# Rotary products of branch B on VectorE, inside the wide gate groups

## The chip, the cores and the metric

The kernel runs on one core of one Trainium2 chip. Its time is the device time of one execution in microseconds; beside it stands the span, from the first to the last instruction of the profiled execution.

## The reference

One layer of a hybrid encoder block on a sequence of 512 rows of width 2048. What matters here is the input projection (10,752 columns) and what branch B does with its eight query heads and two key heads of 128 columns: a norm per head, then a rotary embedding along two axes.

```python
h = rmsnorm(x, norm_g[l])
proj = jnp.einsum('bsd,dc->bsc', h, w_in[l])
qa, ka, va, za, qb, kb, vb, zb, ga, gb = jnp.split(proj, SPLIT_POINTS, axis=-1)
...
qb = axial_rope(rmsnorm(qb.reshape(B, S, N_HEADS_B, DH_B), q_norm_g[l]))
kb = axial_rope(rmsnorm(kb.reshape(B, S, N_KV_B, DH_B), k_norm_g[l]))
ob = gqa_attention(qb, kb, vb)
yb = jnp.einsum('bsc,cd->bsd', ob * jax.nn.silu(zb), w_out_b[l])
merged = jax.nn.sigmoid(ga) * ya + jax.nn.sigmoid(gb) * yb
x = x + jnp.einsum('bsd,de->bse', merged, w_o[l])
```

Branch A (differential attention with its own rotary embedding), the output projections and a final norm complete it; all is float32.

## The kernel before

Every float32 product is made from three matmuls on rounded halves: ScalarE casts a piece of weights to `w_hi` (L115), VectorE computes the residual `w_lo` (L116), and TensorE adds hi x hi, lo x hi and hi x lo. Three buffers of each half (`wp`) let the casts run ahead of TensorE. Large products go by a Strassen scheme of seven products on quarters; the sums of weight quarters are VectorE's (`sub`, L220 and L317), the sums of results too (`plus`, L254 and L337).

The stages in order of time: the input is normed, turned and split; a first part of the projection (L248); then, from about 112 to 570 us, six wide groups of 1024 columns (`strassen_wide`, L329): two keep columns in `pv`, a scratch in HBM, four compute the sigmoid gates (L568) and store them in `gg`. From 570.70 to 764.40 us come the SiLU gates: four groups of 512 columns (`strassen`, L248, L657, L658). Then 16 heads with their attention (from about 764 to 1120 us), between whose steps TensorE takes steps of the rest of the projection and of branch B's output projection, as the list `FILLS` says; then the last projections.

`rope_b(n)` treats one head of branch B (n below 8 a query, 8 and 9 the keys): it loads the head's 512x128 columns from `pv`, ScalarE squares and sums them (L616), GpSimd makes the inverse root with two small operations (`rsqrt_pool`, L111 and L112), then multiplies by the tables and adds (L627 to L629), ScalarE scales the key heads by row (L632), and the columns go back to `pv`. `b_table` multiplies the cosines and signed sines with the norm's gains on GpSimd, once for queries and once for keys (L599, L602). Both tables are made at the start of the SiLU gates, and `to_rope` puts the ten ropes behind the four groups: 4, 3, 3 and 0. The order of instructions on an engine's queue is made by a planner that works from modelled durations; each queue then runs in that order. An instruction under `tc.keep_in_program_order` is put behind the one written before it on its engine; what is written later may still pass it. On TensorE the heads' order is written out by hand. All loads and stores are issued by SyncE's queue.

Of the kernel before, what the change touches and what calls it, by code (L numbers as in the profile page):

```python
# [11 lines left out]
F32 = mybir.dt.float32  # L12
F32R = mybir.dt.float32r
AF = mybir.ActivationFunctionType
ALU = mybir.AluOpType
AX = mybir.AxisListType

P = 128
D = 2048
S = 512  # L20
NT = S // P
NK = D // P
BW = 1024
EPS = 1e-6
# [20 lines left out]
WIDE = "0125"  # L45

FILL_FIRST = 6
FILLS = "130 120 130 120 120 130 130 130 130 130 120 231 231 231 231 231".split()


@with_exitstack
def hybrid_block_kernel(
# [8 lines left out]
    nc = tc.nc  # L61
# [16 lines left out]
    def share_banks(**kw):  # L78
        banks.update(kw)
# [29 lines left out]
    def rsqrt_pool(dst, ss, mul, add, n):  # L109

        nc.gpsimd.tensor_scalar(out=dst, in0=ss, scalar1=mul, scalar2=add, op0=ALU.mult, op1=ALU.add)  # L111
        nc.gpsimd.tensor_tensor(out=dst, in0=dst, in1=neg_half[:, :n], op=ALU.pow)  # L112
# [177 lines left out]
        o = [slots[2 * i:2 * i + 2] for i in range(4)]  # L290
        slots[:] = o[1] + o[0] + o[3] + o[2]

    def strassen_wide(w, left, right, act, wide, done, late=False):

        H = NK // 2

        def load(q, half, pieces):  # L300
            tiles = []
            for p in range(4):
                if q < 2:
                    r = raw_tile(q * 4 + p, (2, S))
                else:
                    r = wide.tile([P, 2, S], F32, name="w_raw", tag=f"w_wide{p}")
                row, at = (half * H + p * 2) * P, 0
                for c0, n in pieces:
                    nc.sync.dma_start(out=r[:, :, at:at + n],
                                      in_=w[row:row + 2 * P, c0:c0 + n].rearrange("(k p) n -> p k n", p=P))  # L310
                    at += n
                tiles.append(r)
            return tiles

        def sub(dst, x0, x1):
            for d, u, v in zip(dst, x0, x1):
                nc.vector.tensor_tensor(out=d, in0=u, in1=v, op=ALU.subtract)  # L317

        def product(name, b):
            ps = acc_tile(2, S)  # L320
            ah, al = act[name]
            for p in range(4):
                hi, lo = split_w(b[p])
                for u in range(2):
                    sl = slice(u * P, (u + 1) * P)
                    for k in range(2):
                        kk = p * 2 + k
                        for i, (l, r) in enumerate(((ah, hi), (al, hi), (ah, lo))):
                            nc.tensor.matmul(out=ps[:, u, :], lhsT=l[:, kk, sl], rhs=r[:, k, :],  # L329
                                             start=kk == 0 and i == 0, stop=kk == H - 1 and i == 2)  # L330
            return ps

        def tmp(tag):
            return wide.tile([P, 2, S], F32, name="wide_" + tag, tag="wide_" + tag)

        def plus(dst, ps, sb):
            nc.vector.tensor_tensor(out=dst, in0=ps, in1=sb, op=ALU.add)  # L337
            return dst

        b11, b12 = load(0, 0, left), None  # L340
        if late:
            b12 = load(1, 0, right)
        b21 = load(2, 1, left)
        b12 = b12 or load(1, 0, right)

        p1 = product("a11", b11)
        u = tmp("u")
        nc.scalar.copy(out=u, in_=p1)
        if not late:
            p2 = product("a12", b21)  # L350
            b22 = load(2, 1, right)
        sub(b11, b12, b11)
        p5 = product("s1", b11)
        if late:
            p2 = product("a12", b21)
            b22 = load(2, 1, right)
        done(0, 0, plus(tmp("c"), p2, u))
        sub(b11, b22, b11)
        p6 = product("s2", b11)
        plus(u, p6, u)  # L360
        t = plus(tmp("t"), p5, u)
        sub(b12, b22, b12)
        p3 = product("s3", b12)
        b21 = load(1, 1, left)
        plus(u, p3, u)
        done(1, 1, plus(tmp("c"), p5, u))
        if late:

            ring = banks["acc"]
            ring[0], ring[1] = ring[1], ring[0]  # L370
        done(0, 1, plus(t, product("s4", b22), t))
        sub(b21, b21, b11)
        done(1, 0, plus(u, product("a22", b21), u))
# [21 lines left out]
    written = {}  # L395
# [42 lines left out]
    with tc.tile_pool(name="xs", bufs=1) as xs:  # L438
# [116 lines left out]
        slots[:] = slots[2:4] + slots[0:2] + slots[4:]  # L555
        new_banks("pair")
        share_banks(acc=[2, 3, 0, 1])
        with tc.tile_pool(name="wide", bufs=1) as wide:
            for n, blocks in enumerate(WIDE_BLOCKS):
                def kept(th, ch, v, blocks=blocks):  # L560
                    keep_cols(blocks[ch * 4:ch * 4 + 4], th * 2, 2, v)

                strassen_wide(w_in, column_pieces(blocks[:4]), column_pieces(blocks[4:]), xq, wide, kept, late=n == 0)


            for g in range(0, 2 * D, 2 * S):
                def merge_gate(th, ch, v, g=g):
                    nc.scalar.activation(out=v, in_=v, func=AF.Sigmoid)  # L568
                    c = g + ch * S
                    nc.sync.dma_start(  # L570
                        out=gg[th * 256:th * 256 + 256, c:c + S].rearrange("(u p) n -> p u n", p=P), in_=v)

                strassen_wide(w_in, [(O_GA + g, S)], [(O_GA + g + S, S)], xq, wide, merge_gate)
        slots[:] = slots[0:2] + slots[4:6] + slots[2:4] + slots[6:8]

        with tc.tile_pool(name="sp", bufs=6) as sp:
# [7 lines left out]
            for blocks in STRASSEN_BLOCKS[1:]:  # L584
                project(blocks, tmp, lambda ps: tmp())

            tabs = {}

            def b_table(nm, src):

                g = sp.tile([P, P], F32, name="g_" + nm, tag="g_" + nm, bufs=1)
                nc.sync.dma_start(out=g, in_=src.broadcast_to([P, P]))
                tcb = sp.tile([P, NT, P], F32, name=f"tc_{nm}", tag=f"tc_{nm}", bufs=1)
                tsb = sp.tile([P, NT, P], F32, name=f"ts_{nm}", tag=f"ts_{nm}", bufs=1)
                nc.sync.dma_start(out=tcb, in_=cos_b.rearrange("(t p) c -> p t c", p=P))
                nc.sync.dma_start(out=tsb, in_=sin_b.rearrange("(t p) c -> p t c", p=P))
                gv = g.rearrange("p (h r j) -> p h r j", h=2, r=2)
                for t in range(NT):
                    nc.gpsimd.tensor_tensor(out=tcb[:, t, :], in0=tcb[:, t, :], in1=g, op=ALU.mult)  # L599
                    ov = tsb[:, t, :].rearrange("p (h r j) -> p h r j", h=2, r=2)  # L600
                    for r in range(2):
                        nc.gpsimd.tensor_tensor(out=ov[:, :, r, :], in0=ov[:, :, r, :],  # L602
                                                in1=gv[:, :, 1 - r, :], op=ALU.mult)
                tabs[nm] = tcb, tsb

            def rope_b(n):


                b = B_QB + n if n < 8 else B_KB + n - 8
                assert written[b] == NT  # L610
                v = sp.tile([P, NT, P], F32, name="cols", tag="cols", bufs=4)
                nc.sync.dma_start(out=v, in_=pv[b])
                sq = sp.tile([P, P], F32, name="bsq", tag="bsq", bufs=1)
                ss = rb[:, n, :]
                for t in range(NT):
                    nc.scalar.activation(out=sq, in_=v[:, t, :], func=AF.Square, accum_out=ss[:, t:t + 1])  # L616
                if n < 8:

                    rsqrt_pool(ss, ss, 1.0, P * EPS, NT)
                else:  # L620
                    rsqrt_pool(ss, ss, 1.0 / P, EPS, NT)
                t2 = sp.tile([P, NT, P], F32, name="rope2", tag="rope2", bufs=1)
                tcb, tsb = tabs["q" if n < 8 else "k"]
                for r in range(2):
                    d, s, m = (x.rearrange("p t (a r j) -> p t a r j", r=2, j=32)[:, :, :, q, :]
                               for x, q in ((t2, r), (v, 1 - r), (tsb, r)))
                    nc.gpsimd.tensor_tensor(out=d, in0=s, in1=m, op=ALU.mult)  # L627
                nc.gpsimd.tensor_tensor(out=v, in0=v, in1=tcb, op=ALU.mult)  # L628
                nc.gpsimd.tensor_tensor(out=v, in0=v, in1=t2, op=ALU.add)  # L629
                if n >= 8:  # L630
                    for t in range(NT):
                        nc.scalar.mul(out=v[:, t, :], in_=v[:, t, :], mul=ss[:, t:t + 1])  # L632
                nc.sync.dma_start(out=pv[b], in_=v)

            b_table("q", q_norm_g)
            b_table("k", k_norm_g)
            to_rope = [(0, 8, 1, 2), (3, 4, 5), (9, 6, 7), ()]


            nc.sync.dma_start(out=sub_g, in_=subln_g.rearrange("o p -> p o"))  # L640
# [12 lines left out]
            for c0, dst in ((O_ZA, zg[0:BW]), (O_ZB, zg[BW:])):  # L653
                for g in range(0, BW, S):
# [8 lines left out]

                    strassen(w_in, c0 + g, c0 + g + 256, xq, False, tmp, gate)
                    for n in to_rope.pop(0):
                        rope_b(n)

    rest = [i for i in range(8) if i not in banks["acc"]]
    share_banks(acc=rest[:2], aux=rest[2:] + banks["acc"])
# [591 lines left out]
```

## Time and profile before

| what | before |
|---|---|
| median of 3 runs | 1397.26 us (1396.12 to 1399.37) |
| the profiled execution's own time | 1396.01 us |
| its span | 1394.2 us |
| mean granted clock of TensorE | 0.988 |
| TensorE busy | 1344.5 us (96%) |
| VectorE busy | 1069.6 us (77%) |
| ScalarE busy | 711.1 us (51%) |
| GpSimd busy | 218.0 us (16%) |

Busy times are of the profiled execution, on the one core. A stage is read from windows of the span: busy time of each engine, and the clock that TensorE was granted in it (1.00 is 2.4 GHz). A wait is put down to what ended it last.

### The profile page before, as it was taken

The numbers are of one execution on the slowest core, as the hardware profiler recorded it, in microseconds if no ns is written. First come the engines' busy times: TensorE is split into PE (matmuls) and PEld (weight loads), VectorE is DVE, ScalarE is ACT, GpSimd is POOL, SyncE is SP. The second block draws the span as 40 slices with busy tenths as digits, with TensorE's granted clock in tenths as the row PEclk, the third lists the DMA queues.
The fourth block names the chain that finished last, engine by engine and source line by source line (L and its number), as shares of the span: only waits on it lengthen the run. The fifth ranks groups of instructions, "written<-read, shape, count | busy, mean of one in ns | idle before, by whom it ended". The sixth has DMA issues, their size and how long they took to land.

```text
span 1394.2 us, 20919 instructions
## 1 busy us (share of the span) xinstructions
PE 1344.5 (96%) x8009; PEld 1200.2 (86%) x8009; DVE 1069.6 (77%) x1271; ACT 711.1 (51%) x1104; POOL 218.0 (16%) x194
## 2 busy tenths in 40 slices
PE   6999999999999999967999999999999999999997
PEld 5998888888888888867999888888889988899997
DVE  5976978778788787736876477978878856799986
ACT  7643343444444444445444476656767733344444
POOL 1000000000000000399100411432220000004322
PEclk9999999999999999987999999999999999999999
DMA  8254653636272734542446684454754455463333
GB/s 287 76 149 134 195 187 116 216 93 240 86 262 91 249 113 146 164 152 98 159 152 173 199 247 129 138 165 144 220 167 153 131 169 187 140 221 112 96 103 121
DMA packets 182756, 222.38 MB, mean 159 GB/s; under 512 B 12016, under 2 KB 126976, under 8 KB 182016
## 3 DMA queue, kind: packets, MB, share of 16 engines
q1 hardware_dynamic: 182656, 221.04, 50.1%
q8 instruction: 63, 1.03, 0.3%
q14 instruction: 37, 0.30, 0.1%
HBM read 181.15 MB, written 35.65 MB: 155 GB/s over the span
## 4 chain that ended last, share of the span: by engine, by line
PE 80%; DVE 6%; POOL 5%; DMA 3%; ACT 3%; issue 3%; SPq 0%; POOLq 0%; DVEq 0%; ACTq 0%
PE acc L329 32%; PE acc L186 21%; PE acc L248 19%; PE aux L762 2%; DVE w_lo L116 2%; PE aux L749 1%; PE aux L875 1%; DMA cols<-pv 1%; POOL rope L627 1%; POOL cols L628 1%; PE aux L805 1%; PE aux L806 1%; POOL cols L629 1%; DMA w_raw<-in_w_in_dram 1%; DMA xt<-in_x_dram 1%
## 5 line engine op out<-in xcount | busy, mean ns | idle before, releaser
L115 ACT CAST w_hi<-w_raw 128x1024 fp32r<-128x1024 f32 x357 | 375.2, 1052 | 479.1 <-PE acc L329 235.5
L116 DVE TENSOR_TENSOR w_lo<-w_raw,w_hi 128x1024 fp32r<-128x1024 f32 x357 | 453.7, 1275 | 189.3 <-ACT w_hi L115 188.9
L317 DVE TENSOR_TENSOR w_raw<-w_raw 128x1024 f32<-128x1024 f32 x96 | 116.8, 1222 | 23.3 <-DMA w_raw<-in_w_in_dram 22.1
L220 DVE TENSOR_TENSOR w_raw<-w_raw 128x1024 f32<-128x1024 f32 x72 | 94.7, 1315 | 3.4 <-DMA w_raw<-in_w_in_dram 2.5
L599 POOL TENSOR_TENSOR tc_q<-tc_q,g_q 128x128 f32<-128x128 f32 x4 | 4.7, 1201 | 556.8 <-DMA g_k<-in_k_norm_g_dram 556.8
L186 PE MATMUL acc<-w_hi,og1h 128*128 128x256 f32 x256 | 73.5, 287 | 2.0 <-DVE rows L939 2.0
L329 PE MATMUL acc<-w_hi,a2h 128*128 128x512 f32 x192 | 74.7, 389 | 0.0
L329 PE MATMUL acc<-w_hi,a2l 128*128 128x512 f32 x192 | 74.7, 389 | 0.0
L329 PE MATMUL acc<-w_lo,a2h 128*128 128x512 f32 x192 | 74.7, 389 | 0.0
L186 PE MATMUL acc<-w_hi,og1l 128*128 128x256 f32 x256 | 73.2, 286 | 0.0
L186 PE MATMUL acc<-w_lo,og1h 128*128 128x256 f32 x256 | 73.1, 286 | 0.0
L716 DVE TENSOR_REDUCE nmax<-aux 128x1 f32<-128x512 f32 x96 | 61.4, 680 | 5.1 <-PE aux L806 5.1
L704 POOL TENSOR_TENSOR cols<-cols,ca 128x512 f32<-128x512 f32 x16 | 23.0, 1435 | 245.2 <-DMA other<-pv 111.4
L186 PE MATMUL acc<-a1h,w_hi 128*128 128x512 f32 (+1 forms) x160 | 56.9, 361 | 0.4 <-ACT a1h L492 0.2
L186 PE MATMUL acc<-a1l,w_hi 128*128 128x512 f32 (+1 forms) x160 | 56.3, 357 | 0.1
L186 PE MATMUL acc<-a1h,w_lo 128*128 128x512 f32 (+1 forms) x160 | 56.3, 356 | 0.0
L186 PE MATMUL acc<-a2h,w_hi 128*128 128x512 f32 (+1 forms) x160 | 55.6, 350 | 0.0
L186 PE MATMUL acc<-a2l,w_hi 128*128 128x512 f32 (+1 forms) x160 | 55.5, 348 | 0.0
L186 PE MATMUL acc<-a2h,w_lo 128*128 128x512 f32 (+1 forms) x160 | 55.4, 347 | 0.0
L186 PEld LDWEIGHTS acc<-w_hi,og1h 128*128 128x128 f32 x256 | 49.7, 194 | 2.8 <-DVE rows L939 2.2
L186 PEld LDWEIGHTS acc<-w_lo,og1h 128*128 128x128 f32 x256 | 49.7, 194 | 0.6
L186 PE MATMUL acc<-w_hi,og0h 128*128 128x512 f32 x128 | 50.0, 392 | 0.0
(360 smaller groups left out, 4102.2 us busy)
## 6 DMA issues: line engine op xcount, KB each, us to landing
w_raw<-in_w_in_dram SPq DMA_DIRECT2D x160, 512.0 KB, 4.5
w_raw<-in_w_in_dram SPq DMA_DIRECT2D x64, 256.0 KB, 4.3
w_raw<-in_w_o_dram SPq DMA_DIRECT2D x32, 512.0 KB, 3.5
cols<-pv SPq DMA_DIRECT2D x36, 256.0 KB, 4.0
w_raw<-in_w_out_b_dram SPq DMA_DIRECT2D x16, 512.0 KB, 3.8
w_raw<-in_w_out_a_dram SPq DMA_DIRECT2D x32, 256.0 KB, 3.2
xt<-in_x_dram SPq DMA_DIRECT2D x8, 512.0 KB, 7.9
gg<-wide_c SPq DMA_DIRECT2D x8, 512.0 KB, 3.6
```

Source lines behind the costliest of these rows:

```text
L115: nc.scalar.copy(out=hi, in_=src)
L116: nc.vector.tensor_tensor(out=lo, in0=src, in1=hi.bitcast(F32), op=ALU.subtract)
L186: nc.tensor.matmul(out=acc[b][:, place], lhsT=l, rhs=r, start=first and kc == order[0] and k == 0 and i == 0, stop=last and kc == order[-1 ...
L220: nc.vector.tensor_tensor(out=d, in0=u, in1=v, op=ALU.subtract)
L248: nc.tensor.matmul(out=ps[u] if by_row else ps[:, u, :], lhsT=l, rhs=r, start=n % (2 if by_row else 4) == 0 and k == 0 and i == 0, stop=n ...
L317: nc.vector.tensor_tensor(out=d, in0=u, in1=v, op=ALU.subtract)
L329: nc.tensor.matmul(out=ps[:, u, :], lhsT=l[:, kk, sl], rhs=r[:, k, :], start=kk == 0 and i == 0, stop=kk == H - 1 and i == 2)
L627: nc.gpsimd.tensor_tensor(out=d, in0=s, in1=m, op=ALU.mult)
L628: nc.gpsimd.tensor_tensor(out=v, in0=v, in1=tcb, op=ALU.mult)
L704: nc.gpsimd.tensor_tensor(out=v, in0=v, in1=ca, op=ALU.mult)
L716: nc.vector.tensor_reduce(out=nmax, in_=sps, axis=AX.X, op=ALU.max, negate=True)
L762: nc.tensor.matmul(out=o, lhsT=l, rhs=r, start=j == 0 and i == 0, stop=j == NT - 1 and i == 2)
```

## The change

The table for queries and the eight query ropes are moved into the four wide gate groups: in each group one rope stands in the middle (`amid`, after the sum `t` is formed and before the weights of `p3` are summed) and one behind it. Only the table and the two ropes for keys stay in the SiLU gates, one behind each of the first two groups. In all ropes the products and the sum run on VectorE instead of GpSimd. The first of them write the two halves of a tile `rope2` that also takes the squares; the squares and the two first products are kept behind what is written before them on their engine. The columns have one buffer instead of four. The list of fill steps for TensorE between the heads is another, with the same total.

```diff
-FILLS = "130 120 130 120 120 130 130 130 130 130 120 231 231 231 231 231".split()
+FILLS = "120 120 130 120 120 130 130 120 120 131 131 231 231 231 231 231".split()
...
     def strassen_wide(w, left, right, act, wide, done, late=False, amid=None):
...
         t = plus(tmp("t"), p5, u)
+        if amid:
+            amid()
         sub(b12, b22, b12)
         p3 = product("s3", b12)
...
+        def rope_b(sp, n):
+            b = B_QB + n if n < 8 else B_KB + n - 8
+            assert written[b] == NT
+            v = sp.tile([P, NT, P], F32, name="cols", tag="cols", bufs=1)
+            nc.sync.dma_start(out=v, in_=pv[b])
+            t2 = sp.tile([P, NT, P], F32, name="rope2", tag="rope2", bufs=1)
+            ss = rb[:, n, :]
+            for t in range(NT):
+                tc.keep_in_program_order(
+                    nc.scalar.activation(out=t2[:, t, :], in_=v[:, t, :], func=AF.Square, accum_out=ss[:, t:t + 1]))
+            if n < 8:
+                rsqrt_pool(ss, ss, 1.0, P * EPS, NT)
+            else:
+                rsqrt_pool(ss, ss, 1.0 / P, EPS, NT)
+            tcb, tsb = tabs["q" if n < 8 else "k"]
+            for r in range(2):
+                d, s, m = (x.rearrange("p t (a r j) -> p t a r j", r=2, j=32)[:, :, :, q, :]
+                           for x, q in ((t2, r), (v, 1 - r), (tsb, r)))
+                tc.keep_in_program_order(nc.vector.tensor_tensor(out=d, in0=s, in1=m, op=ALU.mult))
+            nc.vector.tensor_tensor(out=v, in0=v, in1=tcb, op=ALU.mult)
+            nc.vector.tensor_tensor(out=v, in0=v, in1=t2, op=ALU.add)
+            if n >= 8:
+                for t in range(NT):
+                    nc.scalar.mul(out=v[:, t, :], in_=v[:, t, :], mul=ss[:, t:t + 1])
+            nc.sync.dma_start(out=pv[b], in_=v)
...
+            b_table(wide, "q", q_norm_g)
+            queries = list(range(8))
+            def rope_next():
+                rope_b(wide, queries.pop(0))
             for g in range(0, 2 * D, 2 * S):
...
-                strassen_wide(w_in, [(O_GA + g, S)], [(O_GA + g + S, S)], xq, wide, merge_gate)
+                strassen_wide(w_in, [(O_GA + g, S)], [(O_GA + g + S, S)], xq, wide, merge_gate, amid=rope_next)
+                rope_next()
...
-            b_table("q", q_norm_g)
-            b_table("k", k_norm_g)
-            to_rope = [(0, 8, 1, 2), (3, 4, 5), (9, 6, 7), ()]
+            b_table(sp, "k", k_norm_g)
+            to_rope = [(8,), (9,), (), ()]
```

`b_table(sp, nm, src)` is the function of before, with the pool as an argument.

## Rows read from the trace of the kernel before

**Rows 1.** The page: GpSimd busy, and granted clock, in 40 slices.

```profile
POOL 1000000000000000399100411432220000004322
PEclk9999999999999999987999999999999999999999
```

**Rows 2.** Windows, gates stage: us, busy us (count) by engine, clock, DMA share, GB/s.

```profile
655.00:764.40 109.40, 108.75 (x887) 108.69 (x888) 83.32 (x78) 47.55 (x54) 12.73 (x8) 0.98 0.49 152
sum 193.70, PE 173.72 PEld 171.06 DVE 129.85 ACT 88.22 POOL 85.81; mean PE 57.91 PEld 57.02 DVE 43.28 ACT 29.41 POOL 28.60
```

**Rows 3.** Timeline of TensorE: start us, us, engine line operation.

```profile
571.07 0.28 PE L248 MATMUL acc<-a1h,w_lo 128*128 128x256 f32 x1
571.19 0.28 PE L248 MATMUL acc<-a1h,w_hi 128*128 128x256 f32 x1
...
596.16 0.41 PE L248 MATMUL acc<-s2l,w_hi 128*128 128x256 f32 x1
596.37 0.41 PE L248 MATMUL acc<-s2h,w_lo 128*128 128x256 f32 x1
```

**Rows 4.** Groups, 570 to 765 us, shapes apart: first and last of 18.

```profile
L248 PE MATMUL acc<-a2h,w_lo 128*128 128x256 f32 x128 | 37.1, 290 | 1.6 <-DVE w_lo L116 1.6
...
L248 PE MATMUL acc<-s3h,w_hi 128*128 128x256 f32 x64 | 18.1, 283 | 0.0
```

**Rows 5.** Waits of TensorE, 570.7 to 764.4 us: total, times, longest.

```profile
PE acc L248 <- ACT w_hi L115: 14.5, 5, 5.1
```

**Rows 6.** Waits of ScalarE in the same window.

```profile
ACT bsq L616 <- DMA cols<-pv: 19.7, 4, 9.4
ACT cols L632 <- POOL cols L629: 13.3, 2, 7.1
```

**Rows 7.** Timeline of all engines around 625 us.

```profile
625.06 0.31 ACT L616 ACTIVATE bsq<-cols 128x128 f32<-128x128 f32 x1 [9.41 <-DMA cols<-pv]
...
626.24 1.03 ACT L115 CAST w_hi<-w_raw 128x1024 fp32r<-128x1024 f32 x1
...
627.32 0.58 PE L248 MATMUL acc<-a1h,w_hi 128*128 128x256 f32 x1 [5.14 <-ACT w_hi L115]
```

**Rows 8.** Windows of one wide group, columns as in rows 2.

```profile
413.00:488.00 75.00, 75.00 (x332) 62.12 (x331) 59.04 (x51) 33.67 (x33) 0.00 (x0) 1.00 0.51 164
```

**Rows 9.** Groups in 570 to 765 us, shapes apart: squares and key table.

```profile
L616 ACT ACTIVATE bsq<-cols 128x128 f32<-128x128 f32 x40 | 12.3, 307 | 20.4 <-DMA cols<-pv 19.7
...
L616 ACT ACTIVATION_READ_ACCUMULATOR bsq<-cols 128x1 f32 x40 | 7.5, 187 | 0.0
...
L602 POOL TENSOR_TENSOR ts_k<-ts_k,g_k 128x64 f32<-128x64 f32 x8 | 2.3, 320 | 0.0
L599 POOL TENSOR_TENSOR tc_k<-tc_k,g_k 128x128 f32<-128x128 f32 x4 | 1.7, 461 | 0.0
```

**Rows 10.** VectorE operations with both inputs in SBUF, by group and by timeline.

```profile
L116 DVE TENSOR_TENSOR val<-va,vah 128x512 fp32r<-128x512 f32 x8 | 5.5, 682 | 0.0
...
585.29 0.23 DVE L646 TENSOR_TENSOR lam<-lam 128x64 f32<-128x64 f32 x1 [0.38 <-DMA lam<-in_lambda_k_dram]
```

**Rows 11.** Timeline: a residual and the first matmul that reads it.

```profile
473.55 1.22 DVE L116 TENSOR_TENSOR w_lo<-w_raw,w_hi 128x1024 fp32r<-128x1024 f32 x1
...
476.91 0.39 PE L329 MATMUL acc<-w_lo,s4h 128*128 128x512 f32 x1
```

**Rows 12.** Waits of SyncE's queue over the span.

```profile
SPq L570 <- ACT wide_c L568: 45.5, 8, 9.8
```

**Rows 13.** Timeline: a power on GpSimd and the residual beside it.

```profile
641.55 1.01 POOL L112 TENSOR_TENSOR rb<-rb,neg_half 128x4 f32<-128x4 f32 x1
...
641.72 1.23 DVE L116 TENSOR_TENSOR w_lo<-w_raw,w_hi 128x1024 fp32r<-128x1024 f32 x1 [2.34 <-ACT w_hi L115]
```

**Rows 14.** Heads: a wait of TensorE, and a window (columns as rows 2).

```profile
PE aux L831 <- DVE sql L116: 2.2, 1, 2.2
...
980.00:1000.00 20.00, 19.26 (x108) 16.31 (x108) 16.55 (x30) 14.90 (x31) 5.78 (x4) 0.91 0.73 225
```

More of the change, by code (lines that the diff above doesn't have):

```diff
@@ L291, in strassen, with strassen_wide @@
         slots[:] = o[1] + o[0] + o[3] + o[2]
-    def strassen_wide(w, left, right, act, wide, done, late=False):
+    def strassen_wide(w, left, right, act, wide, done, late=False, amid=None):
         H = NK // 2
@@ L557, in hybrid_block_kernel, with b_table @@
         share_banks(acc=[2, 3, 0, 1])
+        tabs = {}
+        def b_table(sp, nm, src):
+            g = sp.tile([P, P], F32, name="g_" + nm, tag="g_" + nm, bufs=1)
+            nc.sync.dma_start(out=g, in_=src.broadcast_to([P, P]))
+            tcb = sp.tile([P, NT, P], F32, name=f"tc_{nm}", tag=f"tc_{nm}", bufs=1)
+            tsb = sp.tile([P, NT, P], F32, name=f"ts_{nm}", tag=f"ts_{nm}", bufs=1)
+            nc.sync.dma_start(out=tcb, in_=cos_b.rearrange("(t p) c -> p t c", p=P))
+            nc.sync.dma_start(out=tsb, in_=sin_b.rearrange("(t p) c -> p t c", p=P))
+            gv = g.rearrange("p (h r j) -> p h r j", h=2, r=2)
+            for t in range(NT):
+                nc.gpsimd.tensor_tensor(out=tcb[:, t, :], in0=tcb[:, t, :], in1=g, op=ALU.mult)
+                ov = tsb[:, t, :].rearrange("p (h r j) -> p h r j", h=2, r=2)
+                for r in range(2):
+                    nc.gpsimd.tensor_tensor(out=ov[:, :, r, :], in0=ov[:, :, r, :],
+                                            in1=gv[:, :, 1 - r, :], op=ALU.mult)
+            tabs[nm] = tcb, tsb
@@ new lines, in rope_b @@
+        def rope_b(sp, n):
[13 more added lines that the diff above has]
+            tcb, tsb = tabs["q" if n < 8 else "k"]
+            for r in range(2):
+                d, s, m = (x.rearrange("p t (a r j) -> p t a r j", r=2, j=32)[:, :, :, q, :]
[4 more added lines that the diff above has]
+            if n >= 8:
+                for t in range(NT):
+                    nc.scalar.mul(out=v[:, t, :], in_=v[:, t, :], mul=ss[:, t:t + 1])
+            nc.sync.dma_start(out=pv[b], in_=v)
@@ L585, in hybrid_block_kernel @@
                 project(blocks, tmp, lambda ps: tmp())
[L587 to L633, printed above, removed]
@@ L665, in hybrid_block_kernel @@
                     for n in to_rope.pop(0):
-                        rope_b(n)
+                        rope_b(sp, n)
     rest = [i for i in range(8) if i not in banks["acc"]]
```

## The prediction

> **What bounds the kernel now.** I read the 40 slices first: the busy share of GpSimd and the granted clock, to find where the clock of TensorE falls away from its full level. It happens in one place above all, the 18th and 19th slice, which is also the one stretch where GpSimd is busy without a pause [rows 1]. That stretch is the start of the four groups of the SiLU gates (I call it the gates stage), and the windows over it are the second view: from 570.70 to 764.40 us TensorE is busy for 173.72 of 193.70 us, while the last 109.40 us alone hold almost no idle time [rows 2]. The third view is the timeline of TensorE: at full clock the 256-column matmuls of L248 start 0.12 us apart (571.07, 571.19), in the disturbed stretch 0.21 us apart (596.16, 596.37), the lower of the two levels, 1.2 instead of 2.4 GHz, after TensorE had stood still [rows 3]. The fourth view counts the matmuls of the stage: 18 groups of lines, three of 128 and fifteen of 64, together 3 x 128 + 15 x 64 = 1344 [rows 4]. At 0.12 us each they would take 161.3 us. So the gates stage loses 193.7 - 161.3 = **32.4 us**: 20.0 us of idle (193.7 - 173.7) and 12.4 us of slow clock.
>
> Who makes it late? The waits of TensorE name ScalarE's cast L115 first, 14.5 us in five waits [rows 5]. The cast is not slow, it is late, and the waits of ScalarE in the same window say why: its squares L616 stood 19.7 us for the columns that a rope loads, and its row scalings L632 13.3 us for GpSimd's sum L629 [rows 6]. A ScalarE queue runs in order, so every weight cast behind such an instruction stands too. One such chain in full: a square starts at 625.06 after 9.41 us of idle, the cast behind it only at 626.24, and TensorE, idle for 5.14 us, goes on at 627.32 with the half it got [rows 7]. The columns are late because there are four buffers for ten ropes, and a buffer comes free only when GpSimd has finished with it; GpSimd is the slowest link, and SyncE's queue stands behind its stores. In the wide stage before it, by contrast, TensorE is busy for 75.00 of 75.00 us of a group, with VectorE at 59.04 [rows 8].
>
> **The change, part by part.** The sum is made against the profiled execution, 1396.0 us (span 1394.2), which lies 1.3 us under the median of the runs shown, 1397.3.
>
> *Eight query ropes leave the gates stage.* Their loads, squares, GpSimd products and stores go out of it, with the table for the queries. This takes away the GpSimd backlog, and with it the four column waits and the two waits of L632. I take the 32.4 us as gone, less what stays: ropes 8 and 9 (the keys). Each still puts four squares on ScalarE, 4 x (0.307 + 0.187) = 2.0 us, and four scalings, priced like the squares' main part at 0.31, 1.2 us [rows 9], and now about 2.2 us on VectorE (below). Against that, a weight piece here lasts 24 x 0.12 = 2.88 us on TensorE, and its cast starts two pieces ahead (three buffers), 5.76 us, of which cast and residual take some 2.3 (1.03 and 1.22) [rows 7, 11]: about 3.5 us of cover. The new code also pins the squares behind the previous group's last activation, so they come when the columns and the key table are long there. Bounds: nothing, or what ten ropes cost today per rope, 2 x 3.24 = 6.5 us. I take +2, nearer to the lower end because GpSimd is out of the chain.
>
> *The ropes go into the wide groups, two per group.* On VectorE each is two 128x256 products and two 128x512 operations. The 128x512 form with both inputs in SBUF takes 0.68 us, a 128x64 one 0.23 [rows 10]; between them on a line, 128x256 is 0.43 (an estimate from these two rows). One rope is 2 x 0.43 + 2 x 0.68 = 2.2 us, eight are 17.8 us. A group has 75.00 - 59.04 = 16 us of idle on VectorE for 4.5 us of ropes [rows 8], so on average they are hidden. But the first rope of a group is queued behind the sum wide_t, where VectorE works nearly without a gap; what waits behind it are the residuals w_lo of the next product, and TensorE waits for those. The cover is read there: the residual that starts at 473.55 and takes 1.22 is done at 474.77, and the first matmul that reads it starts at 476.91 [rows 11]: 2.1 us, the tightest of the four pieces of that product. So 2.2 us of rope overdraws it by 0.1. Bounds: zero, and all eight ropes in the open, 17.8. I take 0.5 for each first rope, +2 in all, near zero since the residuals run ahead again once the gap-less part is over. ScalarE gets 2.0 us of squares per rope with 41 us idle per group [rows 8]; behind them stand weight casts, which shift by less than the cover.
>
> *Queues.* Eight loads and eight stores of columns and three table loads now stand among the weight loads on SyncE's queue. A store waits for VectorE's last sum, and weight loads stand behind it. The trace has the like: SyncE's stores of gates held that queue for 45.5 us in eight waits, up to 9.8 each [rows 12], with TensorE fully busy [rows 8]. So I cost them at nothing; the cover is the early weight loads, and without it each would cost what exceeds those 9.8 us.
>
> *GpSimd beside VectorE.* The query table is now made during the wide stage: 4 x 0.46 + 8 x 0.32 = 4.4 us of GpSimd work, by the key table's rows that ran undisturbed [rows 9]. If VectorE stood still for all of it, 4.4 us against 2.1 us of cover would cost 2.3; I take +1. Each rope also leaves two small GpSimd operations, the second a power of 1.01 us at 641.55; the residual that started beside it at 641.72 took 1.23, as one does alone [rows 13]. So I add nothing (the other view of it is rival E).
>
> *The fill list.* The total of steps is the same (70 in both lists); heads 0, 7 and 8 lose one step, heads 9 and 10 gain one and two. In head 10 one more step stands before the previous head's norm, whose matmul L831 waits 2.2 us there, after which 20 us run at a granted 0.91 (1.8 us lost) [rows 14]. Bounds: -4.0, or +4 if the heads that lose a step show new holes. I take -2.5.
>
> Sum: 1396.0 - 32.4 + 2 + 2 + 1 - 2.5 = 1366.1, and with the 1.3 us up to the median **1367 us**.
>
> **Rivals.**
> A. *The ropes show in the wide stage.* If the residuals' cover is already used up, all 17.8 us of VectorE work delay TensorE in place of the 2 us taken: 1367 - 2 + 17.8 = 1383. For it: the cover of 2.1 us is no more than one rope. Against: 16 us of idle per group.
> B. *The key ropes keep stalling the gates stage.* Two remain, in the first two groups where all the loss is. At today's rate and with a slow-clock stretch of the kind seen at 596 us behind each (some 2 us), 6.5 + 4 = 10.5 instead of 2: 1376. For it: the parameter sums and two table loads also stand on ScalarE there. Against: no GpSimd product left.
> C. *Slower: ScalarE waits for columns in the wide stage as it does now in the gates stage.* There is one buffer for columns; the next load waits for the last store, and a square that stands for it holds every cast. At 9.41 us [rows 7] less 2.1 of cover, 7.3 each, eight ropes cost 58 us: 1367 - 2 + 58 = 1423. It decides from (32.4 - 2 + 2.5) / 8 = 4.1 us per rope. For it: this wait is the very one of today. Against: ropes are half a group, some 37 us, apart, and the squares are pinned late.
> D. *The change does not do what it says*: the stage loses its time to weight loads or the parameter chain, and the ropes only happen to stand there: 1397. Against: the last 109 us of the stage, nearly free of ropes, have almost no idle [rows 2].
> E. *Each power blocks VectorE.* If a residual stands for the whole 1.01 us of every rope's power, and the cover is already taken by the rope, TensorE loses 8 x 1.0 = 8 us: 1375. Against: the residual of 1.23 us beside the power [rows 13]. The Trainium skill (SBUF — State Buffer, "SBUF: two separate sides") states such a rule: a VectorE operation with two SBUF inputs and a GpSimd operation that reads SBUF shut each other out for a whole instruction; that one row of this trace does not agree with it.
>
> **How the numbers follow.** The likeliest, 0.66, lies between 1361 (nothing stays and the fill list gives all: 1397.3 - 32.4 - 4.0) and 1372 (the key ropes at their upper bound, 4.5 more). A has 0.10, B 0.08, E 0.06, C 0.06, D 0.04. The range 1360 to 1383 takes in the likeliest, A, B and E. A measurement of this kernel tells about 0.2% (2.8 us) from no change. Faster: 0.66 + 0.10 + 0.08 + 0.06 = 0.90; same 0.04 (D); slower 0.06 (C).
>
> **What would show it.** Right: the gates stage in 161 to 168 us, clock near 1.00 in the 18th and 19th slice, GpSimd nearly empty there, no ScalarE wait for columns above 3 us; six wide groups of 75 to 76 us, VectorE near 64 in the last four; L831's wait gone. Wrong: TensorE waiting for w_lo in the last four wide groups (A), for w_hi behind L616 there (C), or for w_hi in the first two gate groups (B).

## The result and the profile after

The changed kernel takes 1364.24 us (median of three runs, 1362.43 to 1366.54) against 1397.26 before: a ratio of 0.9763 [0.9733, 0.9793], 33.0 us less. The forecast was 1367. The profiled execution has a span of 1362.5 us at a mean granted clock of 0.996.

The 40 slices of the page after, GpSimd and granted clock. In the 18th and 19th slice GpSimd falls from 9 and 9 tenths to 1 and 0, and the clock is full [rows 1].

```profile
POOL 1001000000000000010000403413120000004322
PEclk9999999999999999999999999999999999999999
```

Windows over the gates stage after, columns as in [rows 2]: it now ends at 732.3 us, begins at 570.75 as before (570.76), and TensorE is busy for 161.56 of 161.60 us at full clock. GpSimd's busy time there falls from 85.81 [rows 2] to 10.17 us.

```profile
570.70:611.00 40.30, 40.26 (x335) 40.29 (x336) 32.50 (x37) 21.86 (x30) 7.49 (x14) 1.00 0.54 169
...
655.00:732.30 77.30, 77.30 (x645) 77.28 (x644) 57.24 (x57) 34.12 (x41) 0.83 (x1) 1.00 0.48 144
sum 161.60, PE 161.56 PEld 161.56 DVE 125.73 ACT 79.23 POOL 10.17; mean PE 53.85 PEld 53.85 DVE 41.91 ACT 26.41 POOL 3.39
```

Waits of ScalarE in that stage after, the four largest (total us, times, longest). The first row is the healthy one: the cast is early and waits until TensorE frees its buffer. No wait for columns and none for the row scalings is left [rows 6].

```profile
ACT w_hi L115 <- PE acc L248: 65.7, 40, 1.9
ACT w_hi L115 <- issue: 6.5, 5, 1.3
ACT w_hi L115 <- DMA w_raw<-in_w_in_dram: 5.5, 3, 1.8
ACT kept L667 <- DVE kept L666: 3.3, 4, 1.7
```

A wide group after, the same window as [rows 8]. TensorE is still busy throughout, VectorE goes from 59.04 to 62.45 us.

```profile
413.00:488.00 75.00, 75.00 (x332) 62.10 (x331) 62.45 (x59) 36.50 (x49) 2.69 (x4) 1.00 0.54 175
```

So the stages add up: wide stage 0.0 us, gates stage -32.1 (193.6 to 161.5, from its first matmul to the end of its last), heads +0.4 (from there to the last start of the group L186: 1129.0 - 764.4 = 364.6 before, 1097.2 - 732.2 = 365.0 after), together the 31.7 by which the two spans differ.

### The profile page after: what moved, and what is told of

Same layout as the page of the kernel before. It is cut to its first block, busy times and chain, and to the rows that moved or that the text cites. A ratio compares the mean times of both kernels' runs of the same rounds, so it can differ in the third digit from the quotient of the medians.

```text
span 1362.5 us, 20924 instructions
## 1 busy us (share of the span) xinstructions
PE 1331.0 (98%) x8009; PEld 1189.5 (87%) x8009; DVE 1077.3 (79%) x1311; ACT 711.3 (52%) x1105; POOL 157.6 (12%) x154
## 4 chain that ended last, share of the span: by engine, by line
PE 84%; DVE 6%; ACT 3%; DMA 3%; issue 2%; POOL 1%; SPq 0%; POOLq 0%; DVEq 0%; ACTq 0%
PE acc L330 33%; PE acc L248 23%; PE acc L186 20%; PE aux L771 3%; DVE w_lo L116 2%; PE aux L758 1%; DMA rows<-og 1%; PE aux L884 1%; PE aux L814 1%; ACT w_hi L115 1%; PE aux L815 1%; DVE pl L116 1%; DVE nmax L725 1%; ACT p L728 1%; DMA xt<-in_x_dram 1%
## 5 line engine op out<-in xcount | busy, mean ns | idle before, releaser
L116 DVE TENSOR_TENSOR w_lo<-w_raw,w_hi 128x1024 fp32r<-128x1024 f32 x357 | 445.9, 1253 | 151.0 <-ACT w_hi L115 146.0
L318 DVE TENSOR_TENSOR w_raw<-w_raw 128x1024 f32<-128x1024 f32 x96 | 116.1, 1221 | 21.0 <-DMA w_raw<-in_w_in_dram 20.2
L220 DVE TENSOR_TENSOR w_raw<-w_raw 128x1024 f32<-128x1024 f32 x72 | 92.4, 1284 | 0.9
L186 PE MATMUL acc<-w_hi,og1h 128*128 128x256 f32 x256 | 73.6, 288 | 3.5 <-ACT og1h L115 2.3
L186 PE MATMUL acc<-w_hi,og1l 128*128 128x256 f32 x256 | 73.2, 286 | 0.6 <-DVE og1l L116 0.6
L186 PE MATMUL acc<-w_lo,og1h 128*128 128x256 f32 x256 | 73.1, 286 | 0.0
L111 POOL TENSOR_SCALAR rb<-rb 128x4 f32<-128x4 f32 x10 | 3.0, 303 | 493.0 <-ACT rope L591 493.0
L186 PE MATMUL acc<-a1h,w_hi 128*128 128x512 f32 (+1 forms) x160 | 56.4, 357 | 0.2 <-ACT a1h L495 0.2
L186 PE MATMUL acc<-a2h,w_hi 128*128 128x512 f32 (+1 forms) x160 | 55.7, 351 | 0.0
L186 PE MATMUL acc<-a1h,w_lo 128*128 128x512 f32 (+1 forms) x160 | 55.6, 352 | 0.0
L186 PE MATMUL acc<-a2l,w_hi 128*128 128x512 f32 (+1 forms) x160 | 55.5, 348 | 0.0
L186 PE MATMUL acc<-a1l,w_hi 128*128 128x512 f32 (+1 forms) x160 | 55.4, 352 | 0.1
L186 PE MATMUL acc<-a2h,w_lo 128*128 128x512 f32 (+1 forms) x160 | 55.4, 347 | 0.0
L186 PEld LDWEIGHTS acc<-w_hi,og1h 128*128 128x128 f32 x256 | 49.7, 194 | 4.5 <-ACT og1h L115 2.5
L186 PEld LDWEIGHTS acc<-w_hi,og1l 128*128 128x128 f32 x256 | 49.8, 194 | 0.9 <-DVE og1l L116 0.8
L186 PEld LDWEIGHTS acc<-w_lo,og1h 128*128 128x128 f32 x256 | 49.7, 194 | 0.6
L186 PE MATMUL acc<-w_hi,og0h 128*128 128x512 f32 x128 | 50.1, 392 | 0.0
```

The lines of the kernel that those rows point to most:

```text
L116: nc.vector.tensor_tensor(out=lo, in0=src, in1=hi.bitcast(F32), op=ALU.subtract)
L186: nc.tensor.matmul(out=acc[b][:, place], lhsT=l, rhs=r, start=first and kc == order[0] and k == 0 and i == 0, stop=last and kc == order[-1 ...
```

## The experiments

What the result leaves open is which part did it: that the ropes left the SiLU gates (place), that their products left GpSimd (engine), the pinned squares, or the fill list. Each kernel is timed beside the kernel before, whose median was 1395.97 to 1396.64 us there; ratios and differences are to the one beside it. How long the gates stage takes is always counted from its first matmul to the end of its last, in the profiled execution.

**Engine without place: e2.** The kernel before, with only the engine of the rope's products and sums changed.

```diff
-                    nc.gpsimd.tensor_tensor(out=d, in0=s, in1=m, op=ALU.mult)
-                nc.gpsimd.tensor_tensor(out=v, in0=v, in1=tcb, op=ALU.mult)
-                nc.gpsimd.tensor_tensor(out=v, in0=v, in1=t2, op=ALU.add)
+                    nc.vector.tensor_tensor(out=d, in0=s, in1=m, op=ALU.mult)
+                nc.vector.tensor_tensor(out=v, in0=v, in1=tcb, op=ALU.mult)
+                nc.vector.tensor_tensor(out=v, in0=v, in1=t2, op=ALU.add)
```

> The kernel before with only the engine of the ropes' products changed: VectorE instead of GpSimd, all ten ropes and both tables still in the SiLU gates, four buffers, no pins. Theory (what stalls ScalarE is GpSimd's backlog): the stores of columns come early, the waits of the squares and of the row scalings fall from 33.0 us to under 10, the gates stage takes 165 to 175 us instead of 193.7, the time is 1368 to 1380 us. Rival (the place is what counts: ten ropes' squares and loads in two groups are too much, and VectorE, at 32 of 40 us per group, gets 8.8 us more in the first): the stage stays above 180 us and the time above 1384 us.

Measured: 1371.28 us, 0.9819 [0.9802, 0.9836]. All ten ropes are still in the stage, yet it takes 169.2 us instead of 193.6. The engine alone brings 25 of the 33 us, time and stage as its theory had them. In SyncE's queue the stores that waited for GpSimd stood 54.3 us in eight waits in the stage of the kernel before; here they stand 9.5. First the row of before, then that of e2:

```profile
SPq L633 <- POOL cols L629: 54.3, 8, 13.7
```

```profile
SPq L633 <- DVE cols L629: 9.5, 6, 3.9
```

Of the column waits on ScalarE 11.4 us in six are left (longest 3.8, against 9.4 in [rows 6]), a little over the 10 that the theory allowed.

**With the pins as well: e12.** e2, and the pins that the change puts on squares and first products.

```diff
-                    nc.scalar.activation(out=sq, in_=v[:, t, :], func=AF.Square, accum_out=ss[:, t:t + 1])
+                    tc.keep_in_program_order(
+                        nc.scalar.activation(out=sq, in_=v[:, t, :], func=AF.Square, accum_out=ss[:, t:t + 1]))
...
-                    nc.vector.tensor_tensor(out=d, in0=s, in1=m, op=ALU.mult)
+                    tc.keep_in_program_order(nc.vector.tensor_tensor(out=d, in0=s, in1=m, op=ALU.mult))
```

> All ten ropes still in the SiLU gates with their products on VectorE (1371 us without pins, its stage 8 us over the bare rate), now with squares and first products pinned as in the changed kernel. Theory (what was left of the loss there is squares that stand for columns, 11.4 us in six waits): 1364 to 1368 us, so the move into the wide groups adds next to nothing. Rival (the first groups have too little room on VectorE: 3 ropes on top of 32 of 40 us): 1369 us or more, with TensorE waiting for the residual.

Measured: 1364.40 us, 0.9773 [0.9756, 0.9791]; the stage takes 161.8 us with ten ropes in it, and the column waits are gone. The largest wait of ScalarE in the stage, then the only wait of TensorE, at the stage's first matmul:

```profile
ACT w_hi L115 <- PE acc L248: 59.8, 37, 2.1
```

```profile
PE acc L248 <- DVE wide_u L337: 1.7, 1, 1.7
```

This is the time of the changed kernel. The pins bring the 7 us that the engine alone left, and the move into the wide groups adds nothing that these runs can tell.

**Place without engine: e3.** The changed kernel with the three lines of `rope_b` back on `nc.gpsimd`, all ten ropes where the change puts them.

```diff
-                tc.keep_in_program_order(nc.vector.tensor_tensor(out=d, in0=s, in1=m, op=ALU.mult))
-            nc.vector.tensor_tensor(out=v, in0=v, in1=tcb, op=ALU.mult)
-            nc.vector.tensor_tensor(out=v, in0=v, in1=t2, op=ALU.add)
+                tc.keep_in_program_order(nc.gpsimd.tensor_tensor(out=d, in0=s, in1=m, op=ALU.mult))
+            nc.gpsimd.tensor_tensor(out=v, in0=v, in1=tcb, op=ALU.mult)
+            nc.gpsimd.tensor_tensor(out=v, in0=v, in1=t2, op=ALU.add)
```

> The changed kernel with the ropes' products and sums back on GpSimd, all else as changed (query ropes in the wide groups, one buffer, pins). Theory (the place removes the backlog whatever the engine, but a 128x512 operation on GpSimd holds up the residual beside it by about 1 us): GpSimd work of 4.0 us per rope beside residuals with 2.1 us of cover costs TensorE up to 1.9 us per rope in the gap-less part, so 1364 to 1375 us, and wide groups of 75 to 77.5 us. Rival (the engine counts as much as the place, GpSimd anywhere beside full VectorE work stalls TensorE for all of its time): 1364 + 8 x 4 = 1396 us.

Measured: 1418.79 us, 1.0155 [1.0132, 1.0178], slower than before by 22.8 us, and worse than either theory had it. The gates stage starts 43.1 us later (613.85) and takes 173.9 us. So with GpSimd in the chain the place does count: with eight ropes gone the gates stage is 19.7 us shorter than before, but the wide groups lose more than that. Waits of SyncE's queue in the wide groups with ropes, then those of VectorE and TensorE (260 to 640 us):

```profile
SPq L607 <- POOL cols L603: 113.6, 8, 19.2
```

```profile
DVE w_raw L318 <- DMA w_raw<-in_w_in_dram: 43.4, 13, 6.3
...
PE acc L330 <- DVE w_lo L116: 27.1, 7, 5.2
```

Timeline of one such wait:

```profile
355.02 2.15 POOL L603 TENSOR_TENSOR cols<-cols,rope 128x512 f32<-128x512 f32 x1
...
357.20 0.34 SPq L607 DMA_DIRECT2D pv<-cols  x1
359.27 0.33 SPq L586 DMA_DIRECT2D cols<-pv  x1
359.70 2.29 SPq L310 DMA_DIRECT2D w_raw<-in_w_in_dram  x3
364.58 1.23 DVE L318 TENSOR_TENSOR w_raw<-w_raw 128x1024 f32<-128x1024 f32 x1 [6.33 <-DMA w_raw<-in_w_in_dram]
```

The rope's store L607 stands at the head of SyncE's queue until GpSimd's last sum is done; the next column load and three weight loads go out only behind it, and VectorE stands 6.33 us for the weights. That is the queue, not ScalarE, which has no wait for columns in this stretch. Of the 43.1 us TensorE waits 27.1 for residuals; the rest goes with a granted clock of 0.92 to 0.95 in the windows from 338 to 614 us.

**The queue by itself: e5 and e9.** e5 is e3 with the stores of `rope_b` on GpSimd's queue; e9 has the loads there too.

```diff
-            nc.sync.dma_start(out=pv[b], in_=v)
+            nc.gpsimd.dma_start(out=pv[b], in_=v)
```

```diff
-            nc.sync.dma_start(out=v, in_=pv[b])
+            nc.gpsimd.dma_start(out=v, in_=pv[b])
```

> The run with the products on GpSimd in the wide groups, with one line changed: the store of the roped columns is issued from GpSimd's own queue, not from SyncE's. Theory (that run's 55 us over the changed kernel come from SyncE's queue: a store that stands for GpSimd's sum, 113.6 us in 8 waits, keeps weight loads behind it): the wide groups go back to 75 to 78 us, TensorE's waits for the residual fall from 27.1 us to under 8, 1364 to 1380 us. Rival (GpSimd's operations hold up the residuals beside them, whoever stores): 1400 us or more.

> The products on GpSimd in the wide groups, and now both the loads and the stores of the ropes' columns issued from GpSimd's own queue, so that nothing of a rope stands in SyncE's queue. In the run with the store alone moved, SyncE stood 63.6 us at the next column load instead, which waits for the one buffer. Theory (SyncE's queue, with the weight loads behind, carries GpSimd's lateness to TensorE): VectorE's waits for weights in the wide stage fall from 35.6 us to about the 20 of the changed kernel, and the time to 1364 to 1378 us. Rival (GpSimd's operations hold up VectorE's residuals): still 1390 us or more, TensorE waiting for the residual for 10 us or more in the wide stage.

Measured: e5 1404.79 us, 1.0069 [1.0048, 1.0089]; e9 1380.18 us, 0.9879 [0.9863, 0.9894]. e5 has the time of its rival, but not for the rival's reason: more than half of the stand moves to the next load, which has one buffer and waits for the store. Waits of SyncE's queue in e5, then of VectorE in e9, in the same stretch:

```profile
SPq L586 <- DMA pv<-cols: 63.6, 7, 12.4
```

```profile
DVE w_raw L318 <- DMA w_raw<-in_w_in_dram: 15.4, 18, 1.8
```

The start of the gates stage moves from 613.85 (e3) to 599.43 (e5) and 573.82 (e9), against 570.75 in the changed kernel. So 40 of the 43 us that GpSimd cost in the wide groups came through SyncE's queue, and 3 are left for everything else there. In the gates stage of e9 two key ropes on GpSimd still cost 12.8 us (174.3 against 161.5). As a whole e9 is 16.5 us faster than the kernel before, 2 us outside its theory's range: with a queue of its own for the ropes, the move with its pins, without the change of engine, brings half of the gain. GpSimd in the wide groups with more than one buffer for columns was not run.

**The same questions in the kernel before: e4, e6 and e10.** e4 pins the squares only, with the same two lines as the first part of e12's diff. e6 moves only the stores, e10 stores and loads to GpSimd's queue, and e10 pins the squares.

```diff
-                nc.sync.dma_start(out=pv[b], in_=v)
+                nc.gpsimd.dma_start(out=pv[b], in_=v)
```

> The kernel before with only the squares pinned behind what is written before them on ScalarE; ropes and tables where they were, products on GpSimd. Theory (ScalarE stands for GpSimd, whatever the place of the squares): the row scalings still wait for GpSimd's sums and the columns for its buffers, so at least half of the 32 us stays: 1378 to 1397 us. Rival (the squares only came too early in ScalarE's queue, and the pins are what brought the gain): the waits for columns vanish and the time is under 1372 us.

> The kernel before with one line changed: the ropes' stores are issued from GpSimd's own queue. Theory (in the SiLU gates too it is SyncE's queue behind the stores, 54.3 us in 8 waits, that makes columns and weights late, and through the columns ScalarE): the gates stage falls from 193.7 us to under 178, 1365 to 1381 us. Rival as the prediction had it (the columns are late because four buffers come free only as fast as GpSimd works, and the row scalings stand for GpSimd whatever the queue): the stage stays above 186 us and the time above 1388 us.

> The kernel before, products on GpSimd in the SiLU gates, with loads and stores of the ropes' columns on GpSimd's own queue and the squares pinned: neither SyncE's queue nor, but for the row scalings of two heads, ScalarE's stands for GpSimd any more. Theory (the in-order queues of SyncE and ScalarE make the loss, not GpSimd's work as such): stage under 178 us, time under 1381 us. Rival (GpSimd holding up VectorE, or the row scalings alone, or squares that still wait for columns, carry the loss): above 1388 us.

Measured: e4 1392.49 us, 0.9974 [0.9964, 0.9984], stage 187.9, as its theory had it; e6 1403.63 us, 1.0058 [1.0035, 1.0080], stage 201.1, as its rival had it; e10 1385.53 us, 0.9935 [0.9911, 0.9959], stage 181.4. Waits of ScalarE in the stage, of e6 and then of e10:

```profile
ACT cols L632 <- POOL cols L629: 21.3, 2, 12.0
ACT bsq L616 <- DMA cols<-pv: 16.0, 4, 7.3
```

```profile
ACT cols L633 <- POOL cols L630: 14.4, 2, 9.7
```

Taking one of the two waits away does not free TensorE, since the other stays: e4 has no column wait, but its stores still hold SyncE's queue for 63.6 us in eight waits; e6 frees the stores, and the column loads stand instead (41.8 us in six). With both taken away, in e10, about a third of the loss is gone (11.1 of 33.0 us), less than its theory asked for and more than its rival did. What is left there shows in TensorE's waits of e10's stage:

```profile
PE acc L248 <- DVE w_lo L116: 7.2, 7, 1.9
PE acc L248 <- ACT w_hi L115: 6.8, 3, 5.4
```

The scalings that wait for GpSimd stand before the casts, and VectorE is slowed beside GpSimd (residuals of 1.43 us on the mean of the stage against 1.22 in that of the changed kernel). How the 20 us that e10's stage is still too long divide between these, the runs don't show; e10 also puts the issuing of the ropes' DMAs on GpSimd, 0.55 us or more for each. So how GpSimd's lateness reaches TensorE in the SiLU gates stays open for the larger part. More than four column buffers in the SiLU gates were not tried.

**How much room VectorE has: e7 and e8.** The changed kernel with the first two products of every rope issued four and eight times, which makes a rope 4.7 and 8.1 us long.

```diff
-                tc.keep_in_program_order(nc.vector.tensor_tensor(out=d, in0=s, in1=m, op=ALU.mult))
+                for _ in range(4):
+                    tc.keep_in_program_order(nc.vector.tensor_tensor(out=d, in0=s, in1=m, op=ALU.mult))
```

> The changed kernel with the two first products of each rope issued four times each (the same result): 6 x 0.42 = 2.5 us more of VectorE work per rope, 4.7 us in all against 2.2. By the prediction's cover (2.1 us before the residual is needed): 2.6 us beyond it per rope, 8 x 2.6 = 21 us, 1385 us. Rival (the planner puts off the sums of weight quarters that are not yet needed, so the cover is the idle time of a group, 12.5 us for 5 us more): no stall, 1364 to 1367 us.

> The changed kernel with the two first products of each rope issued eight times each: 14 x 0.42 = 5.9 us more of VectorE work per rope, 8.1 us in all. By the prediction's cover: 6 us beyond it per rope, 48 us, 1412 us. Rival (cover is the group's idle time): 11.8 us more per group against 12.5 us left, just hidden or a few us lost, 1364 to 1375 us.

Measured: e7 1368.67 us, 0.9805 [0.9790, 0.9819]; e8 1376.37 us, 0.9865 [0.9848, 0.9881]. Both lie 1 to 2 us above their rival's range and far below what the prediction's cover gave. In e7 no residual is late in the wide stage. In e8 the eight ropes carry 47 us more than in the changed kernel, and the gates stage starts 3.2 us later (573.99); the larger part of its loss, 8.2 us, arises in the gates stage, where the two key ropes carry 12 us more. The window of [rows 8] in e8: VectorE at 70.24 of 75.00 us, TensorE at 74.47.

```profile
413.00:488.00 75.00, 74.47 (x329) 61.34 (x328) 70.24 (x86) 35.85 (x49) 2.82 (x4) 1.00 0.55 171
```

**The pins: e11.** The changed kernel without `keep_in_program_order` around the squares and first products.

```diff
-                tc.keep_in_program_order(
-                    nc.scalar.activation(out=t2[:, t, :], in_=v[:, t, :], func=AF.Square, accum_out=ss[:, t:t + 1]))
+                nc.scalar.activation(out=t2[:, t, :], in_=v[:, t, :], func=AF.Square, accum_out=ss[:, t:t + 1])
```

> The changed kernel without the pins on the squares and the two first products. Theory (the engine and the place do the work; VectorE keeps up, so a square that floats ahead finds its columns soon): 1364 to 1369 us. Rival (unpinned squares float ahead in ScalarE's queue and stand for columns with the casts behind them, as they did before the change): ScalarE waits of 10 us or more for columns, 1372 us or more.

Measured: 1367.65 us, 0.9791 [0.9775, 0.9807]. Waits of ScalarE from 260 to 740 us:

```profile
ACT rope L590 <- DMA cols<-pv: 21.3, 8, 4.1
```

The squares do stand for columns now, once per rope, but for 2.7 us on the mean, and TensorE waits only 0.9 us for residuals in that stretch. The gates stage starts 2.4 us later. The interval overlaps that of the changed kernel, so the pins' 3 us here are not told from nothing; with the ropes still in the SiLU gates they were worth 7 (e2 against e12).

**The fill list: e1.** The changed kernel with the list of before.

```diff
-FILLS = "120 120 130 120 120 130 130 120 120 131 131 231 231 231 231 231".split()
+FILLS = "130 120 130 120 120 130 130 130 130 130 120 231 231 231 231 231".split()
```

> The changed kernel with the list of fill steps of before. Theory (the list is worth nothing, since the heads took 361.6 us in the profile of before and 362.1 in the profile after): 1364 us, within 2 us, and heads of 361 to 362 us. Rival (the prediction's term, -2.5 us for the list, hidden after by something else that the ropes' move costs the heads): 1366 to 1367 us, with TensorE's wait at the norm's matmul back at about 2 us.

Measured: 1362.19 us, 0.9752 [0.9732, 0.9772], no difference from the changed kernel. Waits of TensorE in the heads, of the changed kernel and then of e1:

```profile
PE acc L186 <- ACT og1h L115: 2.3, 1, 2.3
```

```profile
PE aux L840 <- DVE sql L116: 2.1, 1, 2.1
```

The norm's wait [rows 14] goes with the new list and comes back with the old one (as L840, by the changed line numbers), but under the new list another of its size stands for it, and a window of 20 us at a granted 0.91 follows there too (960 to 980 us).

## Why the prediction was right, and where it was not

**The 32.4 us of the gates stage: right in size.** 161.3 us were counted, 161.5 measured. TensorE's idle time and its slow clock are both gone. The cause was told only half right. That GpSimd is the slow link, and that ScalarE's waits for columns and scalings pass its lateness on, the waits of before show. But the text made the gain out of ropes that "leave the gates stage". With VectorE in the chain they need not leave it: e12 has all of the gain with the ropes still there. Nor is leaving enough: without the change of engine the move, pins included, takes 19.7 us off the gates stage and costs more than it brings (e3), or, with the ropes' DMAs off SyncE's queue, brings half (e9). So the change of engine, with the pins, is what is sufficient, and with it the place makes no difference that these runs can tell. SyncE's queue, named in half a sentence, is one of the ways by which GpSimd's lateness travels, and in the wide groups nearly the only one (e3, e5, e9).

**Key ropes, +2: 0.2.** Nothing of them is seen: after, TensorE's only wait in the stage is at its first matmul (1.7 us, as before). With GpSimd in the chain the two ropes cost 12.8 (e9), above the 10.5 of rival B, which named this place.

**Wide ropes, +2: 0.** The size of the operations was near: the 128x256 product takes 0.42 us, estimated 0.43 (the line between the two rows gives 0.42). The cover was misread. The 2.1 us came from the residuals of one product in the order before, but VectorE's other work in that stretch is not all equally due. Timeline of VectorE after, at the first rope of a group:

```profile
465.34 0.75 DVE L601 TENSOR_TENSOR rope<-cols,ts_q 128x256 f32<-128x256 f32 x2
466.01 1.22 DVE L116 TENSOR_TENSOR w_lo<-w_raw,w_hi 128x1024 fp32r<-128x1024 f32 x1
467.14 0.69 DVE L602 TENSOR_TENSOR cols<-cols,tc_q 128x512 f32<-128x512 f32 x1
...
468.88 0.69 DVE L603 TENSOR_TENSOR cols<-cols,rope 128x512 f32<-128x512 f32 x1
469.48 1.22 DVE L318 TENSOR_TENSOR w_raw<-w_raw 128x1024 f32<-128x1024 f32 x1
...
476.29 2.36 DVE L318 TENSOR_TENSOR w_raw<-w_raw 128x1024 f32<-128x1024 f32 x2
```

The residuals stand between the rope's operations, and it is the sums of raw weights for later products (L318) that are put off. So the cover is a group's idle time, 75.0 - 62.4 = 12.6 us after the change, and not 2.1 per rope: by the prediction's reading e8 would have lost 8 x (8.1 - 2.1) = 48 us, and its wide stage lost 3.2.

**Queues, 0: right for this change, wrong as a rule.** The ropes' stores hold SyncE's queue for 29.8 us in ten waits, up to 5.2, and TensorE shows no wait from it. Those of e3 hold it for 113.6 us in eight, up to 19.2, and cost 40. The prediction's row [rows 12] marks the safe side, with eight waits of up to 9.8. By these rows it is the length of one wait that counts, and with it how slow the engine is that the store waits for; a limit between 9.8 and 19.2 was not measured.

**Query table, +1: 0.** It ran in the first wide group (125.39 to 131.39 us) without a wait of TensorE, though it took 6.0 us and not 4.4. **The power, 0: right.** Timeline after, a power and the rope's product beside it: the product takes its 0.69 us as one does alone [rows 10].

```profile
497.58 1.06 POOL L112 TENSOR_TENSOR rb<-rb,neg_half 128x4 f32<-128x4 f32 x1
...
497.82 0.69 DVE L602 TENSOR_TENSOR cols<-cols,tc_q 128x512 f32<-128x512 f32 x1
```

**Fill list, -2.5: +0.4** in the heads, and e1 tells no difference. The wait was there to be taken, but another one took its place; a gain read from one wait holds only if the next work is ready.

Against the sum, the key ropes came out 1.8 us lower, wide ropes and query table together 3.0 lower, and the heads 2.9 higher. That these nearly cancel is luck, and it is why 1367 lies so close to 1364.

**The rivals.** D fell with the result. A needed VectorE full; e8 shows that it begins to show near 70 us of a group's 75. C's wait appears in e11, at a longest of 4.1 us instead of 9.4, with a store that now waits for VectorE; e3, which has the slow engine, came near C's time, 1419 against 1423, but through SyncE's queue and not ScalarE. E did not occur.

## What to carry to other kernels

Before moving work to another place, ask whether the place or the engine makes it late: a helper chain on a slow engine can cost through every in-order queue that has an instruction waiting for it, the DMA issuer's included, and freeing one queue can hand the wait to the next. Cover is read from what can be put off, not from the nearest deadline: repeating an instruction four and eight times measures it. A wait that is seen in one place is a gain only if what comes behind it is ready.

## What the runs showed of the hardware

GpSimd's and VectorE's operations on SBUF delay each other. Timeline of e3, beside the sum shown above:

```profile
352.03 6.23 DVE L116 TENSOR_TENSOR w_lo<-w_raw,w_hi 128x1024 fp32r<-128x1024 f32 x3
352.79 2.15 POOL L602 TENSOR_TENSOR cols<-cols,tc_q 128x512 f32<-128x512 f32 x1
```

Three residuals, where VectorE's operations of this size start 1.13 us apart while GpSimd is still (466.01 and 467.14 in the timeline of the changed kernel above), take 6.23 us here, and each of the two GpSimd operations, the product and the sum, 2.15; alone such a one takes 1.3 (1.30 us at 620.11 in the kernel before, where VectorE stands still). 3 x 1.13 + 2 x 1.3 = 6.0, so the two engines' times add up as if only one worked at a time. The Trainium skill (SBUF — State Buffer, "SBUF: two separate sides") says just that of a VectorE operation with two SBUF inputs and a GpSimd operation that reads SBUF: the one that starts first shuts the other out for its whole instruction. For these operations the trace agrees.

For the power on 128x4 values it agrees in one direction only, and the prediction had read one power of ten [rows 13]. In the kernel before, four of the ten begin while a residual is under way and take 1.99 to 2.00 us, the others 1.01 to 1.02:

```profile
653.85 1.74 DVE L116 TENSOR_TENSOR w_lo<-w_raw,w_hi 128x1024 fp32r<-128x1024 f32 x1 [5.93 <-ACT w_hi L115]
654.47 1.99 POOL L112 TENSOR_TENSOR rb<-rb,neg_half 128x4 f32<-128x4 f32 x1
```

The other way round, a VectorE operation that begins 0.17 us (641.72 in [rows 13]) or 0.24 us (497.82 above) into a power is not held up; there the trace differs from the page.

A DMA issue also takes longer on GpSimd's queue, 0.64 us for a rope's store (e9, 432.06 us) against 0.34 on SyncE's (e3, above).
